# Part of the down projection as seven block products instead of eight, with wide weight tiles

## The chip, the cores and the metric

The kernel runs on one core of one Trainium2 chip. The metric is device microseconds of one execution of the whole program. The matrix engine is TensorE (PE, with its weight loads as PEld), VectorE is DVE, ScalarE is ACT, GpSimd is POOL, SyncE is SP. SP issues almost all transfers of this kernel.

## The reference, cut to what matters

Two layers of an encoder on 256 tokens of width 2048, all in float32. The change sits in the last line of a layer:

```
x = x + mixed @ w_o
x = x + (silu(g) * u) @ w_down          # [g | u] = DWConv3(RMSNorm(x) @ w_up)
```

`w_up` is 2048 x 11264 and `w_down` is 5632 x 2048 for each layer. So the down projection contracts 44 tiles of 128 features, for two tiles of 128 tokens (m = 0, 1) and four column blocks of 512 (c = 0 to 3).

## The kernel before, in words

**Products.** TensorE takes float32r operands. To keep float32 accuracy each operand is split in a rounded part (hi) and the rest (lo), and a product is three matmuls: activation hi by weight hi, activation lo by weight hi, activation hi by weight lo. `rows_by_cols` (L163) does this for one block of four 128-feature tiles by 512 columns: 4 x 2 x 3 = 24 matmuls of 128x512 into two PSUM banks, one for each token tile.

**Weights.** `split_weights` (L113) loads such a block, 1 MB, into a `raw` tile (SP, L119), makes its hi with ScalarE (L127) and its lo with VectorE, raw minus hi (`lo_part`, L111). hi and lo tiles hold 1024 columns, so a block has two of each. There are 3 raw tiles, 4 hi and 4 lo: two blocks of hi and lo, one being used and one being made. All this is urgent: the framework's scheduler puts it in its engine's queue as early as the tiles come free, and every engine then works through its queue in order. A transfer into a raw tile waits until the lo that reads the tile's old content is done; a hi or lo waits until TensorE has used the tile's old content.

**The feed-forward part.** Its 5632 features go in two halves of 24 and 20 tiles (loop at L845). For a half, `gate_and_up` (L814) takes four feature tiles at a time: four `w_up` blocks for g and four for u; the rows leave PSUM through ScalarE (`leave`, L794), are transposed by four DMA transposes on SP (L809), joined (L381), convolved (L781 to L785), gated (L827) and split in hi and lo (L242, L243) into the list `ys`, one tile of 2 KB for each feature tile. Then the down projection of that half runs at L855 to L866: for each c, one pair of PSUM banks, all blocks of the half in order, then `residual` (L560) adds the result to `xr`. The last transposes and convolutions of a half lie beside the first blocks of its down projection. `let_in` (L156) admits the steps that wait for them at the second tile of every block.

Other tiles (`sl`) come from a pool of 58 tiles of 2 KB; PSUM has three double banks (`mm`) and two single ones (`tp`).

Of the kernel before, what the change touches and what calls it, by code (L numbers as in the profile page):

```python
# [8 lines left out]
F32 = mybir.dt.float32  # L9
# [25 lines left out]

C_N1, C_AG, C_SG, C_N2, C_CW = 0, 16, 24, 32, 48
# [6 lines left out]
def encoder(ctx: ExitStack, tc: tile.TileContext, xT, x, w_in, w_gu, w_o, w_up, w_down, wsT, pcol, prow, rope, out):  # L43
# [4 lines left out]
    slots = pool("slots", 58)  # L48
    evp = pool("evp", 4)
    rawp = pool("rawp", 3)  # L50
    hip = pool("hip", 4)
    lop = pool("lop", 4)
# [56 lines left out]

    def lo_part(lo, part, hi):  # L110
        nc.vector.tensor_tensor(out=lo, in0=part, in1=hi.bitcast(F32), op=ALU.subtract)  # L111

    def split_weights(src, loaded=None, later=None, step=2 * W):  # L113
        n = src.shape[-1]
        with urgent():
            raw = loaded
            if raw is None:
                raw = rawp.tile([P, 4 * W], F32, tag="raw", name="raw")
                nc.sync.dma_start(raw[:, :n], src)  # L119
            his, los = [], []  # L120
            for h in range(0, n, 2 * W):
                hi = hip.tile([P, 2 * W], F32R, tag="hi", name="hi")
                lo = lop.tile([P, 2 * W], F32R, tag="lo", name="lo") if later is None else None
                for a in range(0, 2 * W, step):
                    part = raw[:, h + a : h + a + step]
                    cs = slice(a, a + step)
                    nc.scalar.activation(hi[:, cs], part, AF.Copy)  # L127
                    if later is None:
                        lo_part(lo[:, cs], part, hi[:, cs])
                    else:  # L130
                        later.append((part, hi[:, cs]))
                his.append(hi)
                los.append(lo)
        return his, los


    def split_later(later):
        los = []
        with urgent():
            for part, hi in later:  # L140
                lo = lop.tile([P, 2 * W], F32R, tag="lo", name="lo")
                lo_part(lo, part, hi)
                los.append(lo)
        return los
# [18 lines left out]
    def rows_by_cols(ps, acts, src, first, last, raw=None, apart=False):  # L163

        his, los = split_weights(src, raw, None, 2 * W if raw is None else W)

        def product(m, kk, part):
            cs = slice(kk % 2 * W, (kk % 2 + 1) * W)
            w = (his if part < 2 else los)[kk // 2][:, cs]
# [19 lines left out]

    def take(steps):  # L190
        for step in steps:
            with tc.issue_after(latest()):
                step()


    def unit(acts, w, steps=()):
        ps = mm()
        his, los = [], []
        for b in range(0, NK, UB):
            h, lo = split_weights(w[:, b * UW : (b + UB) * UW])  # L200
            his += h
            los += lo

        def tile_of(tiles, k, i):
            c = k % KB * UW + i * P
            return tiles[k // KB][:, c : c + P]
# [362 lines left out]
    for l in range(DEPTH):  # L569
# [244 lines left out]
        def gate_and_up(j, ys):  # L814
# [5 lines left out]
            def up_in(tall):  # L820
                for i in range(2):
# [6 lines left out]
                    for k in range(2):  # L828
                        ys.append(split_plain(y[:, k, :]))

# [14 lines left out]
        for f0, f1 in ((0, 24), (24, NF)):  # L845
            ys = []
            for j in range(f0 // 4, f1 // 4):
                gate_and_up(j, ys)
# [6 lines left out]
            for c in range(4):  # L855
                end = last and not more and c == 3
                ps = [tp([P, W]) for _ in range(2)] if end else (lambda t: [t[:, m, :] for m in range(2)])(mm())
                for k in range(f0, f1, KB):
                    src = w_down[l, c, :, k * W : (k + KB) * W]
                    rows_by_cols(ps, ys[k - f0 : k - f0 + KB], src, k == f0, k + KB == f1, None, end and k + KB == f1)  # L860
                if not (last and not more):
# [4 lines left out]
                    continue  # L866
                for m in range(2):
                    step = W // 2 if end and m else W
                    for a in range(0, W, step):
# [3 lines left out]
                        (nc.scalar if end and a else nc.sync).dma_start(out[:, m, c * W + a : c * W + a + step], to)  # L873

# [56 lines left out]
```

## Time and profile before

| | |
|---|---|
| time, median of 3 runs | 1972.02 us (1971.8 to 1972.1) |
| the profiled execution | 1971.57 us, of which its span is 1969.8 us |
| PE, busy | 1963.6 us |
| ACT, busy | 1316.6 us |
| DVE, busy | 1256.4 us |
| POOL, busy | 22.6 us |
| HBM read | 378.43 MB |

The span is what the profile covers, from the first instruction to the last; 1.8 us of the execution lie outside it. Busy time is the union of an engine's instructions. A row of the groups gives line, engine, operation, output and input, shapes and count, then busy time and mean of one, then the idle time just ahead of these instructions and what ended it.

### The profile page before, as it was taken

The page shows a single profiled execution, that of the slowest core. Times are in us where ns is not written, and L with a number is a line of the kernel's source. Part 1 is how long each engine was busy: PE and PEld are TensorE (multiplying, and loading weights), DVE is VectorE, ACT ScalarE, POOL GpSimd, SP SyncE. Part 2 cuts the span into 40 slices and gives each one's busy share as a digit, 9 for nine tenths or more (in the row PEclk, how much of TensorE's full clock was granted, in tenths as well). Part 3 has the DMA queues.
Part 4 walks back from the last instruction along what each step waited for, and adds up shares of the span by engine and source line. Part 5 has one row for each costly group of instructions (what it writes and reads, how often), then busy time and mean ns, then how long its engine had stood idle before and what let it go on. Part 6 is the DMA issues. An engine that isn't in the chain of part 4 may idle for free.

```text
span 1969.8 us, 23916 instructions
## 1 busy us (share of the span) xinstructions
PE 1963.6 (100%) x8880; PEld 1630.6 (83%) x8880; DVE 1256.4 (64%) x1754; ACT 1316.6 (67%) x1685; POOL 22.6 (1%) x25
## 2 busy tenths in 40 slices
PE   9999999999999999999999999999999999999999
PEld 8888888888888888888888888888888888888887
DVE  6779776666664456666567796666666544666664
ACT  6687487877753477777666864787777435777742
POOL 0100000000000000000000000000000000000000
PEclk9999999999999999999999999999999999999999
DMA  9764687777755677776667456867776556678763
GB/s 342 205 204 150 205 239 202 222 219 228 216 198 192 199 215 204 229 221 205 215 204 248 141 178 203 235 206 218 232 218 219 193 192 203 213 216 217 220 216 126
DMA packets 190741, 414.09 MB, mean 210 GB/s; under 512 B 139424, under 2 KB 140704, under 8 KB 145568
## 3 DMA queue, kind: packets, MB, share of 16 engines
q1 hardware_dynamic: 189904, 411.83, 67.2%
q8 instruction: 69, 1.13, 0.2%
q10 hardware_dynamic: 720, 0.73, 0.1%
q14 instruction: 48, 0.39, 0.1%
HBM read 378.43 MB, written 2.10 MB: 193 GB/s over the span
## 4 chain that ended last, share of the span: by engine, by line
PE 97%; DVE 2%; issue 0%; DMA 0%; SPq 0%; POOL 0%; ACT 0%; DVEq 0%
PE mm L170 91%; PE mm L211 2%; PE tp L170 1%; PE mm L216 1%; DVE lo L111 1%; PE tp L254 0%; PE tp L256 0%; PE tp L255 0%; PE tp L697 0%; PE tp L482 0%; DMA raw<-in_w_in 0%; DVE sl L235 0%; DVE xr L562 0%; SPq L87 0%; DVE sl L265 0%
## 5 line engine op out<-in xcount | busy, mean ns | idle before, releaser
L170 PE MATMUL mm<-hi,sl 128*128 128x512 f32 x5296 | 1418.4, 389 | 0.8 <-DVE sl L243 0.6
L111 DVE TENSOR_TENSOR lo<-raw,hi 128x1024 fp32r<-128x1024 f32 (+1 forms) x708 | 856.5, 1217 | 627.6 <-ACT hi L127 616.7
L170 PEld LDWEIGHTS mm<-hi,sl 128*128 128x128 f32 x5296 | 992.7, 188 | 208.2 <-DVE sl L243 1.5
L127 ACT ACTIVATE hi<-raw 128x1024 fp32r<-128x1024 f32 (+1 forms) x708 | 739.9, 1051 | 461.5 <-PE mm L170 426.0
L170 PE MATMUL mm<-lo,sl 128*128 128x512 f32 x2648 | 816.1, 389 | 0.0
L170 PEld LDWEIGHTS mm<-lo,sl 128*128 128x128 f32 x2648 | 496.9, 188 | 103.1
L381 ACT COPY sl<-sl 128x1024 uint16<-128x1024 uint16 x98 | 132.1, 1351 | 119.3 <-DMA sl<-sl 119.2
L781 ACT ACTIVATE sc<-sl,pc 128x256 f32<-128x256 f32 x176 | 97.0, 588 | 0.0
L801 ACT COPY sl<-ev 128x1024 uint16<-128x1024 uint16 x88 | 89.5, 1037 | 0.0
L782 DVE SCALAR_TENSOR_TENSOR sc<-sl,pc,sc 128x255 f32<-128x255 f32 x176 | 79.1, 479 | 2.6 <-ACT sc L781 2.6
L785 DVE SCALAR_TENSOR_TENSOR sc<-sl,pc,sc 128x255 f32<-128x255 f32 x176 | 79.1, 480 | 1.6
L211 PE MATMUL mm<-sl,hi 128*128 128x512 f32 x256 | 62.0, 391 | 0.0
L211 PEld LDWEIGHTS mm<-sl,hi 128*128 128x128 f32 x256 | 47.3, 188 | 9.3
L799 ACT ACTIVATE ev<-mm,yr 128x512 f32<-128x512 f32 x88 | 54.8, 672 | 0.0
L235 DVE SCALAR_TENSOR_TENSOR sl<-sl,pc 128x256 fp32r<-128x256 f32 x96 | 42.5, 479 | 16.9 <-ACT sl L234 16.9
L242 ACT ACTIVATE sl<-sl 128x256 fp32r<-128x256 f32 x88 | 32.1, 410 | 27.9 <-DVE sl L827 27.4
L234 ACT ACTIVATE sl<-sl,pc 128x256 fp32r<-128x256 f32 x96 | 43.0, 496 | 1.2 <-DMA pc<-in_pcol 0.6
L535 ACT COPY sl<-sl 128x1024 uint16<-128x1024 uint16 x24 | 32.4, 1349 | 6.8 <-DMA sl<-sl 6.8
L216 PE MATMUL mm<-sl,lo 128*128 128x256 f32 x256 | 34.2, 285 | 0.0
L243 DVE TENSOR_TENSOR sl<-sl 128x256 fp32r<-128x256 f32 x88 | 33.3, 419 | 0.0
L216 PEld LDWEIGHTS mm<-sl,lo 128*128 128x128 f32 x256 | 32.4, 191 | 0.6
L827 DVE TENSOR_TENSOR sl<-sl,sc 128x512 f32<-128x512 f32 x44 | 30.2, 686 | 0.2
(112 smaller groups left out, 582.7 us busy)
## 6 DMA issues: line engine op xcount, KB each, us to landing
raw<-in_w_up SPq DMA_DIRECT2D x176, 1024.0 KB, 5.0
raw<-in_w_down SPq DMA_DIRECT2D x88, 1024.0 KB, 4.9
raw<-in_w_in SPq DMA_DIRECT2D x38, 1024.0 KB, 5.3
raw<-in_w_o SPq DMA_DIRECT2D x32, 1024.0 KB, 5.0
raw<-in_w_gu SPq DMA_DIRECT2D x16, 1024.0 KB, 5.1
sl<-sl SPq DMA_TRANSPOSE x244, 3.6
sl<-in_prow SPq DMA_DIRECT2D x12, 256.0 KB, 7.0
raw<-in_w_in SPq DMA_DIRECT2D x8, 256.0 KB, 4.9
```

The costliest lines, as they stand in the source:

```text
L111: nc.vector.tensor_tensor(out=lo, in0=part, in1=hi.bitcast(F32), op=ALU.subtract)
L127: nc.scalar.activation(hi[:, cs], part, AF.Copy)
L170: nc.tensor.matmul(ps[m], acts[kk][:, part % 2, m * P : (m + 1) * P], w, start=first and kk == 0 and part == 0, stop=last and kk == KB - 1 ...
L211: nc.tensor.matmul(ps[:, i, :], tile_of(his, k, i), x1, start=k == 0, stop=False)
L216: nc.tensor.matmul(ps[:, i, :SEQ], tile_of(los, k, i), acts[k][:, 0, :], start=False, stop=k == NK - 1)
L234: nc.scalar.activation(t[:, 0, :], src, AF.Copy, scale=g)
L381: nc.scalar.copy(words, tall.rearrange("p (b a) n -> p b (a n)", b=2))
L781: nc.scalar.activation(t[:, i, :], s[:, i, :], AF.Identity, bias=col(3), scale=col(1))
L782: nc.vector.scalar_tensor_tensor(out=t[:, i, 1:], in0=s[:, i, : SEQ - 1], scalar=col(0), in1=t[:, i, 1:], op0=ALU.mult, op1=ALU.add)
L785: nc.vector.scalar_tensor_tensor(out=t[:, i, : SEQ - 1], in0=s[:, i, 1:], scalar=col(2), in1=t[:, i, : SEQ - 1], op0=ALU.mult, op1=ALU.add)
L799: nc.scalar.activation(rows, ps[:, m, :], AF.Copy, scale=r2[:, m : m + 1])
L801: nc.scalar.copy(h, rows.bitcast(U16).rearrange("p (j n b) -> p j b n", j=2, b=2))
```

## The change

**Seven products for eight.** Two feature tiles (k, k+1) by two token tiles by two column blocks (c, c+1) are eight block products, that is 24 matmuls. After the change some of these groups are done as seven products of sums and differences (the Winograd form of Strassen's scheme), 21 matmuls, in the new function `seven`. The halves are now 20 and 24 feature tiles. Column blocks are taken in pairs; in both pairs of the first half three groups, in the first pair of the second half four groups are done in this way, in the second pair of the second half none: ten a layer, twenty in all. All other blocks (`direct`) are as before, with 4 feature tiles, or 2 where the count leaves a rest.

**Sums of weights.** A group needs its weights and four sums of them. Of the four weight blocks (here named by their place in the row of `w_down`: 0, 1, 2, 3) three are loaded into a raw tile, the fourth twice into a second raw tile `sums`; a transfer issued by GpSimd then adds blocks 1 and 2 from HBM to these two copies as it writes (`accum_op`), and VectorE makes the other two sums. So a group has a hi and a lo of 1536 columns and another hi and lo of 2048. The host orders `w_down` so that each block's or group's weights are contiguous in a row.

**Sums of activations.** `mixed` makes four combinations of the two token tiles by two feature tiles, with three VectorE instructions, and splits them into hi and lo: seven times a layer.

**Results.** Four of the seven products go to four more PSUM banks (one `mm` and the two `tp`), which add up over all groups of a pair; `seven_out` combines them at the end of the pair's last group, with one ScalarE copy and seven VectorE instructions, into `xr`.

**Tiles.** hi and lo are 2048 columns wide everywhere, three of each (24 KB each for a partition, 16 KB before); raw tiles are four; `sl` tiles are 48. Outside the first two blocks of the program hi and lo are made with one instruction each for 2048 columns.

```diff
+HALVES = ((0, 20), (20, NF))
+FAST = ((4, 8, 14), (4, 8, 14, 18))
...
+    plain = [k for k in range(f0, f1) if k - f0 - (k - f0) % 2 not in fast]
+    out = []
+    for i in range(0, len(plain), KB):
+        ks = tuple(plain[i : i + KB])
+        own = [((c[0],), ks, False), ((c[1],), ks, False)]
+        if i // KB < len(fast):
+            k = f0 + fast[i // KB]
+            own.insert(1 if i + KB < len(plain) else 0, (c, (k, k + 1), True))
+        out += own
...
-    slots = pool("slots", 58)
+    slots = pool("slots", 48)
...
-    rawp = pool("rawp", 3)
-    hip = pool("hip", 4)
-    lop = pool("lop", 4)
+    rawp = pool("rawp", 4)
+    hip = pool("hip", 3)
+    lop = pool("lop", 3)
...
-    def split_weights(src, loaded=None, later=None, step=2 * W):
+    def split_weights(src, loaded=None, step=4 * W):
...
+            hi, lo = hi_tile(), lo_tile()
+            for a in range(0, n, step):
+                cs = slice(a, min(a + step, n))
+                nc.scalar.activation(hi[:, cs], raw[:, cs], AF.Copy)
+                lo_part(lo[:, cs], raw[:, cs], hi[:, cs])
...
+    def mixed(y):
+        t = y.rearrange("p a (m t) -> p (a m) t", t=P)
+        e = ev().rearrange("p a (m t) -> p (a m) t", t=P)
+        a21 = t[:, 1:2, :].to_broadcast([P, 2, P])
+        nc.vector.tensor_tensor(out=e[:, 0:2, :], in0=a21, in1=t[:, 0:4:3, :], op=ALU.subtract)
+        nc.vector.tensor_tensor(out=e[:, 2, :], in0=t[:, 0, :], in1=e[:, 1, :], op=ALU.subtract)
+        nc.vector.tensor_tensor(out=e[:, 3, :], in0=t[:, 2, :], in1=e[:, 2, :], op=ALU.subtract)
+        return parts(e.rearrange("p a t -> p (a t)"), [P, W])
+
+    def seven(left, right, more, acts, mix, src, used_left, used_right, first, last):
+        with urgent():
+            raw, sums = raw_tile(), raw_tile()
+            nc.sync.dma_start(raw[:, : 3 * W], src[:, : 3 * W])
+            s = sums.rearrange("p (g c) -> p g c", c=W)
+            b12 = src[:, 3 * W :].unsqueeze(1).to_broadcast([P, 2, W])
+            nc.sync.dma_start(s[:, :2, :], b12)
+            nc.gpsimd.dma_start(sums[:, : 2 * W], src[:, W : 3 * W], accum_op=ALU.add)
+            hi, lo, his, los = hi_tile(), lo_tile(), hi_tile(), lo_tile()
+            nc.scalar.activation(hi[:, : 3 * W], raw[:, : 3 * W], AF.Copy)
+            b = raw.rearrange("p (g c) -> p g c", c=W)
+            nc.vector.tensor_tensor(out=s[:, 2, :], in0=s[:, 0, :], in1=b[:, 2, :], op=ALU.add)
+            nc.vector.tensor_tensor(out=s[:, 3, :], in0=s[:, 2, :], in1=b[:, 0, :], op=ALU.add)
+            nc.scalar.activation(his, sums, AF.Copy)
+            lo_part(lo[:, : 3 * W], raw[:, : 3 * W], hi[:, : 3 * W])
+            lo_part(los, sums, his)
...
+        for ps, used, m, a, w, g in (
+            (left, used_left, 0, own(1, 0), (hi, lo), 0),
+            (right, used_right, 0, mix_of(3), (hi, lo), 2),
+            (more, used_more, 0, own(0, 0), (hi, lo), 1),
+            (more, used_more, 1, mix_of(2), (his, los), 2),
+            (more, used_more, 2, mix_of(1), (his, los), 0),
+            (more, used_more, 3, mix_of(0), (his, los), 1),
+            (left, used_left, 1, own(1, 1), (his, los), 3),
+        ):
+            cs = slice(g * W, (g + 1) * W)
+            new = m not in used
+            used.add(m)
+            nc.tensor.matmul(ps[m], a[0], w[0][:, cs], start=new, stop=False)
+            nc.tensor.matmul(ps[m], a[1], w[0][:, cs], start=False, stop=False)
+            nc.tensor.matmul(ps[m], a[0], w[1][:, cs], start=False, stop=ps is more and last)
...
-        for f0, f1 in ((0, 24), (24, NF)):
-            ys = []
+        for half, (f0, f1) in enumerate(HALVES):
+            ys, mixes = [], {}
...
+            for group in range(2):
+                fast = sevens(half, group)
+                blocks = down_blocks(half, group)
+                sums, fresh = {}, {}
...
+        "w_down": down(a(w_down)),
```

**Where the order moves: SP, start of the first half's down projection, layer 0.** SP's queue from the last `w_up` load on. Before, `raw_4684`, `raw_4722`, `raw_4756` and `raw_4790` are the first four down blocks; the transposes are those of the last up blocks.

```order
L119 DMA raw_4684<-in_w_down 128x2048
L809 DMA_TRANSPOSE sl_4526<-sl_4520 128x4x128
L809 DMA_TRANSPOSE sl_4526<-sl_4524 128x4x128
L809 DMA_TRANSPOSE sl_4527<-sl_4520 128x4x128
L809 DMA_TRANSPOSE sl_4527<-sl_4524 128x4x128
L119 DMA raw_4722<-in_w_down 128x2048
L119 DMA raw_4756<-in_w_down 128x2048
L119 DMA raw_4790<-in_w_down 128x2048
```

Now, `raw_4094` and `raw_4124` are the second and third direct block, `raw_4154` the weights of the second group of seven; `raw_4059` and `raw_4155` are the sums of the first and second group.

```order
L249 DMA raw_4059<-in_w_down 128x2x512
L918 DMA_TRANSPOSE sl_3878<-sl_3872 128x4x128
L918 DMA_TRANSPOSE sl_3879<-sl_3872 128x4x128
L918 DMA_TRANSPOSE sl_3878<-sl_3876 128x4x128
L918 DMA_TRANSPOSE sl_3879<-sl_3876 128x4x128
L156 DMA raw_4094<-in_w_down 128x2048
L156 DMA raw_4124<-in_w_down 128x2048
L246 DMA raw_4154<-in_w_down 128x1536
L918 DMA_TRANSPOSE sl_4017<-sl_4011 128x4x128
L918 DMA_TRANSPOSE sl_4018<-sl_4011 128x4x128
L249 DMA raw_4155<-in_w_down 128x2x512
L918 DMA_TRANSPOSE sl_4017<-sl_4015 128x4x128
```

Both sums stand in the same raw tile: `raw_4155` takes the place of `raw_4059`, and its transfer waits for the lo that is made of `raw_4059`. Two transposes of the last up block now stand ahead of it on SP.

**VectorE, the same place.** Before, the los of the first down blocks stand in a row, each waiting for its hi alone.

```order
L111 TENSOR_TENSOR lo_4687<-raw_4684,hi_4686 128x1024
L111 TENSOR_TENSOR lo_4691<-raw_4684,hi_4690 128x1024
L111 TENSOR_TENSOR lo_4725<-raw_4722,hi_4724 128x1024
L111 TENSOR_TENSOR lo_4729<-raw_4722,hi_4728 128x1024
L111 TENSOR_TENSOR lo_4759<-raw_4756,hi_4758 128x1024
```

Now, from the second group's sums on, in the order of the queue:

```order
L254 TENSOR_TENSOR raw_4155<-raw_4155,raw_4154 128x512
L148 TENSOR_TENSOR lo_4160<-raw_4154,hi_4159 128x1536
L255 TENSOR_TENSOR raw_4155<-raw_4155,raw_4154 128x512
L891 SCALAR_TENSOR_TENSOR sc_4219<-sl_4208,pc_89,sc_4219 128x255 x2
L894 SCALAR_TENSOR_TENSOR sc_4219<-sl_4208,pc_89,sc_4219 128x255 x2
L891 SCALAR_TENSOR_TENSOR sc_4236<-sl_3995,pc_89,sc_4236 128x255
L936 TENSOR_TENSOR sl_4210<-sl_4210,sc_4219 128x512
L894 SCALAR_TENSOR_TENSOR sc_4236<-sl_3995,pc_89,sc_4236 128x255
L148 TENSOR_TENSOR lo_4162<-raw_4155,hi_4161 128x2048
```

L254 is the first instruction that needs the accumulating transfer; the los behind it wait with it, and six convolution rows and a gating row (L936) stand ahead of the lo of the sums.

**VectorE, third and fourth group of the second half, first pair (layer 1; layer 0 has the same order).** `raw_14361` and `raw_14427` are the sums of the third and fourth group; `lo_14399` is the lo of the one direct block that TensorE does between them.

```order
L254 TENSOR_TENSOR raw_14361<-raw_14361,raw_14360 128x512
L148 TENSOR_TENSOR lo_14366<-raw_14360,hi_14365 128x1536
L255 TENSOR_TENSOR raw_14361<-raw_14361,raw_14360 128x512
L148 TENSOR_TENSOR lo_14368<-raw_14361,hi_14367 128x2048
L254 TENSOR_TENSOR raw_14427<-raw_14427,raw_14426 128x512
L148 TENSOR_TENSOR lo_14399<-raw_14396,hi_14398 128x2048
L255 TENSOR_TENSOR raw_14427<-raw_14427,raw_14426 128x512
L148 TENSOR_TENSOR lo_14432<-raw_14426,hi_14431 128x1536
```

The fourth group's first sum stands ahead of the lo of the direct block that comes before that group on TensorE. `raw_14427` takes the place of `raw_14360`, so its transfer waits for the third group's L255 and `lo_14366`.

156 lines of the change are left out of this document (115 added, 41 removed).

## The prediction

> **What bounds the kernel now.** I read the head of the page first, with the chain that ended last.
>
> ```profile
> PE 1963.6 (100%) x8880; PEld 1630.6 (83%) x8880; DVE 1256.4 (64%) x1754; ACT 1316.6 (67%) x1685; POOL 22.6 (1%) x25
> ...
> PE 97%; DVE 2%; issue 0%; DMA 0%; SPq 0%; POOL 0%; ACT 0%; DVEq 0%
> ```
>
> TensorE is busy all the time and is the chain. A busy TensorE need not be at its pace, so the next view is the chain in order of time in an undisturbed stretch, then the busy time in a stretch of the first down projection.
>
> ```profile
> 299.88 160.25 PE mm L170 x707
> ```
>
> ```profile
> 520.00:640.00 120.00, 120.00 (x531) 99.37 (x531) 68.32 (x74) 59.99 (x67) 0.00 (x0) 1.00 0.61 205
> ```
>
> A matmul of 128x512 takes 160.25 / 707 = 0.2267 us, and the down projection has the same pace: 120.00 / 531 = 0.226. The columns after it are PEld, DVE (57%), ACT (50%), POOL, the granted clock (1.00), the share of the DMA engines (0.61) and GB/s. No other engine is near its limit there. The waits tell how the feeding works.
>
> ```profile
> DVE lo L111 <- ACT hi L127: 616.7, 399, 6.2
> ACT hi L127 <- PE mm L170: 426.0, 302, 2.6
> ...
> SPq L119 <- DVE lo L111: 1212.1, 258, 14.6
> ```
>
> SP waits for a raw tile, ScalarE for TensorE to give a hi back, VectorE for ScalarE. These waits are slack: everything is made a block ahead. So fewer matmuls shorten the program, and anything that uses up the slack lengthens it.
>
> **The matmuls taken away.** Each group of seven has 21 matmuls for 24; twenty groups take away 60, 60 x 0.2267 = 13.6 us. Nothing else runs on TensorE for it. This is all that can be won.
>
> **Work added on the other engines.** The means by shape:
>
> ```profile
> L111 DVE TENSOR_TENSOR lo<-raw,hi 128x1024 fp32r<-128x1024 f32 x700 | 851.1, 1223 | 625.5 <-ACT hi L127 614.7 <-PE mm L170 9.8 <-PE mm L216 0.4
> L127 ACT ACTIVATE hi<-raw 128x1024 fp32r<-128x1024 f32 x700 | 734.8, 1056 | 459.6 <-PE mm L170 426.0 <-PE tp L170 10.0 <-PE mm L211 6.7
> ...
> L560 DVE TENSOR_TENSOR xr<-mm,xr 128x512 f32<-128x512 f32 x24 | 15.5, 686 | 10.7 <-PE mm L170 10.7
> ...
> L111 DVE TENSOR_TENSOR lo<-raw,hi 128x512 fp32r<-128x512 f32 x8 | 5.4, 692 | 2.0 <-ACT hi L127 2.0
> ...
> L127 ACT ACTIVATE hi<-raw 128x512 fp32r<-128x512 f32 x8 | 5.1, 633 | 1.9 <-DMA raw<-in_w_in 1.8
> ```
>
> 512 more columns cost a lo 1.223 - 0.692 = 0.53 us and a hi 0.42 us. So a lo of 1536 columns takes 1.75, of 2048 2.29; a hi of 1536 takes 1.48, of 2048 1.90; a sum of 128x512 takes 0.69. In the steady pattern (a group, two direct blocks) TensorE needs (21 + 48) x 0.2267 = 15.64 us. VectorE does 2 x 2.29 for the blocks and 2 x 0.69 + 1.75 + 2.29 for the group, 10.0 us or 64%; ScalarE 2 x 1.90 + 1.48 + 1.90 = 7.2 us, 46%. The transfers write 2 x 1024 KB and 768 + 512 + 512 KB, 251 GB/s beside the 205 at share 0.61 above, so about 0.75. Nobody is full. The four instructions of `mixed` on VectorE (14 x at most 4 x 0.69) and the seven of `seven_out` (six times, 5.4 us) lie beside matmuls; I cost them at nothing. If that cover failed at the six ends of a pair, TensorE would wait at most for the PSUM banks, but a direct block of 5.4 us always stands between.
>
> **The chain of a group's sums** is what has no cover by rule: a transfer into `sums` (call it B), the accumulating transfer (A), L254, the lo of 1536 columns where it stands between, L255, the hi (1.90), the lo (2.29); and only then may the next group's B start, in the same tile. That is A + B + 0.69 + 1.75 + 0.69 + 1.90 + 2.29 = A + B + 7.32 against TensorE's 15.64. Neither A nor B is in the trace. The nearest rows:
>
> ```profile
> raw<-in_w_down SPq DMA_DIRECT2D x88, 1024.0 KB, 4.9
> ...
> sl<-sl SPq DMA_TRANSPOSE x244, 3.6
> ...
> xr<-in_x SPq DMA_DIRECT2D x2, 1024.0 KB, 9.3
> out_x<-xr SPq DMA_DIRECT2D x7, 256.0 KB, 2.8
> ```
>
> Between 256 KB in 2.8 and 1024 KB in 4.9 us, B's 512 KB are at 3.5. A moves 512 KB too, but reads its destination beside its source: between 3.5 (as if plain) and 4.9 (the reading of 1 MB), I take 4.2. A + B = 7.7. From below they can't be under two transfers of 256 KB, 5.6; from above A could be as slow as the `xr` loads among other traffic, 9.3, and the sum 12.8.
>
> The Trainium skill, "DMA: Bandwidth & Descriptors", section "Anatomy of one DMA — SWDGE (gpsimd) path", gives a transfer issued by GpSimd 2.0 us and its bytes at 436 GB/s; for 512 KB that is an estimate of 3.2, A + B would be 6.7, and the forecast below about 1960. No run here shows it, and the page doesn't say that its fit covers accumulation.
>
> **Where the chain meets TensorE.** Let D be the end of the half's last up block. The two places rest on these rows:
>
> ```profile
> 532.02 5.95 SPq L809 DMA_TRANSPOSE sl<-sl  x4
> ```
>
> ```profile
> L801 ACT COPY sl<-ev 128x1024 uint16<-128x1024 uint16 x88 | 89.5, 1037 | 0.0
> L782 DVE SCALAR_TENSOR_TENSOR sc<-sl,pc,sc 128x255 f32<-128x255 f32 x176 | 79.1, 479 | 2.6 <-ACT sc L781 2.6
> ...
> L799 ACT ACTIVATE ev<-mm,yr 128x512 f32<-128x512 f32 x88 | 54.8, 672 | 0.0
> ...
> L827 DVE TENSOR_TENSOR sl<-sl,sc 128x512 f32<-128x512 f32 x44 | 30.2, 686 | 0.2
> ```
>
> First group: its B takes an up block's tile, free four blocks of 5.44 ahead of D and 1.90 + 2.29 later, D - 17.6; the sums are there before D. Its hi waits for TensorE until D, its lo is done at D + 4.2 and wanted at D + 5.44 + 2.5: no wait. Second group: B stands on SP behind two transposes (1.49 each) whose source ScalarE makes after the first group's hi (D + 1.90), two rows of 0.67 and one of 1.04: it starts at D + 7.3. Landed with A + B at 15.0; L254, lo, L255 to 18.1; six convolution rows and a gating row, 3.6, to 21.7; lo to 23.95. TensorE reaches the group at 5.44 + 4.76 + 10.88 = 21.1 and needs this lo eleven matmuls later, at 23.6. It waits 0.4 us, in four halves: 1.5. Third group: its lo is ready 15.0 after the second's, TensorE comes 15.64 after: no wait. In the first halves the later groups have more room (four short blocks lie between the third and fourth).
>
> Third to fourth group of the second half: one direct block lies between, and the order puts L254 of the fourth group ahead of that block's lo. Queued behind this L254 are that lo and all that VectorE does next, and TensorE waits for the lo at once. B may start when the third group's L255 is done, 10.8 after the second group's lo; A + B = 7.7, L254 0.69, lo 2.29: 21.5. TensorE wants it at 2.27 + 10.88 + 4.76 + 0.91 = 18.8. It waits 2.7, in two layers: 5.4.
>
> **Wide tiles at the start.** The first block after the two preloaded ones is fed straight from its transfer:
>
> ```profile
> 15.10 1.06 ACT L127 ACTIVATE hi<-raw 128x1024 fp32r<-128x1024 f32 x1 [1.69 <-DMA raw<-in_w_in]
> ...
> 16.84 1.07 PE L170 MATMUL mm<-hi,sl 128*128 128x512 f32 x4
> ...
> 17.75 0.62 PE L170 MATMUL mm<-lo,sl 128*128 128x512 f32 x2
> ```
>
> Hi would be done at 15.10 + 1.90 = 17.0, lo at 19.3, used at 17.75 before: 1.5 us late. Later blocks have three tiles instead of two blocks' worth, so more lead; I cost them at nothing.
>
> **Sum.** -13.6 + 1.5 + 1.5 + 5.4 = -5.2 us. The profiled execution took 1971.57 us (span 1969.8), 0.45 below the median of the runs; I take the difference from the median, 1972.0: 1966.8 us, 0.26% less. A difference of 0.2%, 3.9 us, is about what a measurement of this kernel can tell from none.
>
> **Rivals.**
>
> *The accumulating transfer is slow and becomes the bound; slower.* With x = A + B, the wait at the second group is x - 7.3 (four times), at the third x - 8.3 (four times), at the block between third and fourth x - 4.4 (twice). At x = 8.3 all is given back; at x = 10, 10.8 + 6.8 + 11.2 + 1.5 - 13.6 = +16.7, 1988.7; at the upper bound 12.8 it would be about 2017. For it: the four raw loads round A share the engines with it, and nothing in the trace accumulates. Against it: the share of 0.61 leaves room. Chance 0.26.
>
> *Given back, no change.* x between 7.9 and 8.7, inside my own uncertainty: 1968 to 1976. Chance 0.17.
>
> *GpSimd is held up by VectorE.* The trace has a sign of it:
>
> ```profile
> 56.08 2.99 POOL L271 TENSOR_TENSOR kr<-kv,mhalf 128x4 f32<-128x4 f32 x1 [2.74 <-DVE kv L269]
> ...
> 151.50 0.70 POOL L679 TENSOR_TENSOR lnr<-lnv,mhalf 128x2 f32<-128x2 f32 x1 [54.55 <-DVE rec L470]
> ```
>
> ```profile
> 56.12 0.42 DVE L388 TENSOR_TENSOR sl<-sl 128x256 f32<-128x256 f32 x1
> 56.45 1.22 DVE L111 TENSOR_TENSOR lo<-raw,hi 128x1024 fp32r<-128x1024 f32 x1
> ```
>
> A tiny instruction on GpSimd took 2.99 instead of 0.70 us while VectorE worked with two inputs from SBUF. If preparing a transfer is held up so, A grows by 2.3, x is 10.0: 1988.7. The Trainium skill, "SBUF — State Buffer", section "SBUF: two separate sides", has this as a trap for transfers issued by GpSimd, but for VectorE's two-port modes; its section "Who interferes with whom" says that an instruction with two SBUF inputs holds up GpSimd's reads, not its writes. By that rule the trace agrees with the row above and A stays as it is. Chance 0.06.
>
> *The attention loses.* Order and tiles change there (48 for 58), and VectorE is fuller:
>
> ```profile
> 1010.00:1170.00 160.00, 159.62 (x819) 135.44 (x818) 122.42 (x224) 114.12 (x174) 8.54 (x5) 1.00 0.59 191
> ```
>
> If four wide los a layer stood where one of half the width stood ahead of a step that TensorE waits for, 4 x 1.06 x 2 = 8.5 us: 1975.3. Against: TensorE idles 0.4 us of 160 there now. Chance 0.04.
>
> **How the numbers follow.** My forecast has 0.47; "faster" is this case, "same" is the second rival, 0.17; "slower" the other three, 0.36. The range goes from no wait at all, 1972.0 - 13.6 = 1958.4, to x = 10, 1988.7; above it lie the worst of the accumulation, about one in ten.
>
> **What would show it.** PE with 8820 matmuls at 0.227. A row of GpSimd's transfers with the time to landing, near 4.2, and of the 512 KB loads, near 3.5. VectorE's L254 waiting for a transfer; TensorE waiting for lo in each half's second group, under half a us, and some 3 us between the third and fourth group of the second halves. Near 14 us the start, with 1.5 us lost. I am wrong if TensorE waits elsewhere, or if L254 never waits.

## The result, and the profile after

The changed kernel takes 2081.5 us (median; 2076.8 to 2085.0) against 1971.9 of the kernel before on the same chip: a ratio of 1.0555, interval 1.0536 to 1.0573, 5.6% slower. The prediction was 1966.8, its range ended at 1988.7. The profiled execution of after took 2084.99 us, its span is 2083.2.

The head of the page of after and its chain that ended last:

```profile
PE 1997.3 (96%) x8820; PEld 1633.4 (78%) x8820; DVE 1326.1 (64%) x1566; ACT 1305.6 (63%) x1379; POOL 37.1 (2%) x45
...
PE 5%; DMA 1%; DVE 1%; issue 0%; ACT 0%; SPq 0%; DVEq 0%; ACTq 0%; POOLq 0%
```

The 60 matmuls are gone (8820), but TensorE is busy 33.7 us longer than before and idle for 85.9 us (2083.2 - 1997.3) where it was 6.2. So there are two losses: some 80 us of waiting, and 33.7 + 13.6 = 47 us of slower matmuls. VectorE and ScalarE are far from full, 64% and 63%.

Where it is lost, by busy time in four stretches of after: a down projection, the up projection behind it, and two more down projections, each cut at TensorE's first matmul of a stage. The columns are length, PE, PEld, DVE, ACT, POOL, granted clock, DMA share, GB/s.

```profile
497.70:627.80 130.10, 115.40 (x463) 91.04 (x463) 85.11 (x82) 63.08 (x54) 4.35 (x5) 0.93 0.69 212
627.80:899.70 271.90, 264.86 (x1154) 215.25 (x1153) 162.34 (x178) 180.17 (x187) 0.85 (x1) 1.00 0.69 202
899.70:1048.70 149.00, 135.58 (x566) 109.64 (x565) 90.59 (x83) 88.99 (x88) 2.62 (x3) 0.93 0.71 221
...
1534.20:1665.30 131.10, 114.75 (x463) 91.34 (x462) 87.25 (x84) 64.11 (x54) 4.30 (x5) 0.93 0.69 211
```

463 matmuls at 0.2267 us are 105.0 us: the first half's down projection needs 25 more, with 14.7 us of idle time and a mean clock of 0.93. But the up projection, which holds no group, takes 271.9 for 1154 x 0.2267 = 261.6 too, at full clock; in the other layer (1665.2 to 1930.0) it takes 264.8.

The waits of after, for VectorE, ScalarE and TensorE (us in all, times, longest):

```profile
DVE raw L254 <- DMA raw<-in_w_down: 118.5, 20, 10.6
```

```profile
ACT sl L490 <- DMA sl<-sl: 218.6, 47, 8.4
...
ACT hi L256 <- DVE raw L255: 128.8, 16, 10.9
```

```profile
PE mm L281 <- DVE lo L148: 34.7, 14, 4.4
PE mm L214 <- DVE lo L148: 21.6, 11, 6.9
PE mm L187 <- DVE lo L148: 18.2, 20, 2.0
```

VectorE's first sum waits for the transfer in all twenty groups, ScalarE's hi of the sums stands behind it, and TensorE waits for lo: in groups (L281), in direct blocks (L214), and in the stages outside the down projection, the up projections above all (L187), where no sum is made.

The transfers of after, with the median from issue to landing:

```profile
raw<-in_w_down SPq DMA_DIRECT2D x64, 1024.0 KB, 5.3
...
raw<-in_w_down SPq DMA_DIRECT2D x20, 768.0 KB, 4.2
raw<-in_w_down SPq DMA_DIRECT2D x28, 512.0 KB, 3.8
raw<-in_w_down POOLq DMA_DIRECT2D x20, 512.0 KB, 7.8
```

A loop of the sums, the second group of the first half, in the timelines of SP, GpSimd, VectorE and TensorE. Its load B was issued at 508.08, its transfer A at 512.62.

```profile
508.08 0.52 SPq L249 DMA_DIRECT2D raw<-in_w_down  x1
...
531.20 0.38 SPq L249 DMA_DIRECT2D raw<-in_w_down  x1
...
554.35 0.38 SPq L249 DMA_DIRECT2D raw<-in_w_down  x1
```

```profile
512.62 0.87 POOL L250 DMA_DIRECT2D raw<-in_w_down  x1 [22.55 <-DMA raw<-in_w_down]
```

```profile
523.05 0.69 DVE L254 TENSOR_TENSOR raw<-raw 128x512 f32<-128x512 f32 x1 [10.30 <-DMA raw<-in_w_down]
523.65 1.75 DVE L148 TENSOR_TENSOR lo<-raw,hi 128x1536 fp32r<-128x1536 f32 x1
525.32 0.68 DVE L255 TENSOR_TENSOR raw<-raw 128x512 f32<-128x512 f32 x1
...
528.90 2.28 DVE L148 TENSOR_TENSOR lo<-raw,hi 128x2048 fp32r<-128x2048 f32 x1
```

```profile
520.95 0.39 PE L280 MATMUL mm<-hi,sl 128*128 128x512 f32 x1
525.46 0.67 PE L281 MATMUL mm<-lo,sl 128*128 128x512 f32 x1 [4.13 <-DVE lo L148]
525.92 0.63 PE L279 MATMUL mm<-hi,sl 128*128 128x512 f32 x1
...
531.23 0.50 PE L281 MATMUL mm<-lo,sl 128*128 128x512 f32 x1 [1.86 <-DVE lo L148]
531.57 0.40 PE L279 MATMUL tp<-hi,sl 128*128 128x512 f32 x1
```

From B to A 4.5 us, from A to L254 10.4, from L254 to the end of the last lo 8.1: then the next B goes out (531.20), 23.1 us after the one before, where TensorE needs 15.64 for a group and two blocks. This is the prediction's loop, at A + B = 15.0. TensorE waits 4.13 us for the lo of 1536 columns, though its hi was done at 515.4: it stands behind the late sum on VectorE.

### The profile page after: what moved, and what is told of

It is laid out like the page before. It is cut to its first block, busy times and chain, and to the rows that moved or that the text cites. A ratio compares the mean times of both kernels' runs of the same rounds, so it can differ in the third digit from the quotient of the medians.

```text
span 2083.2 us, 22991 instructions
## 1 busy us (share of the span) xinstructions
PE 1997.3 (96%) x8820; PEld 1633.4 (78%) x8820; DVE 1326.1 (64%) x1566; ACT 1305.6 (63%) x1379; POOL 37.1 (2%) x45
## 3 DMA queue, kind: packets, MB, share of 16 engines
q8 instruction: 69, 1.13, 0.2%
## 5 line engine op out<-in xcount | busy, mean ns | idle before, releaser
L148 DVE TENSOR_TENSOR lo<-raw,hi 128x2048 fp32r<-128x2048 f32 (+3 forms) x382 | 839.7, 2204 | 421.8 <-ACT hi L160 396.0
L187 PE MATMUL mm<-hi,sl 128*128 128x512 f32 x3968 | 1067.0, 390 | 3.3 <-ACT hi L160 3.1
L187 PEld LDWEIGHTS mm<-hi,sl 128*128 128x128 f32 x3968 | 743.1, 188 | 161.6 <-ACT hi L160 7.2
L160 ACT ACTIVATE hi<-raw 128x2048 fp32r<-128x2048 f32 (+2 forms) x342 | 635.1, 1861 | 323.3 <-PE mm L187 190.1
L187 PE MATMUL mm<-lo,sl 128*128 128x512 f32 x1984 | 615.0, 391 | 18.3 <-DVE lo L148 18.2
L187 PEld LDWEIGHTS mm<-lo,sl 128*128 128x128 f32 x1984 | 370.3, 188 | 104.2 <-DVE lo L148 28.9
L214 PE MATMUL mm<-hi,sl 128*128 128x512 f32 x992 | 271.4, 396 | 0.0
L490 ACT COPY sl<-sl 128x1024 uint16<-128x1024 uint16 x98 | 129.5, 1347 | 218.6 <-DMA sl<-sl 218.6
L214 PEld LDWEIGHTS mm<-hi,sl 128*128 128x128 f32 x992 | 190.2, 192 | 41.7 <-ACT hi L160 1.0
L214 PE MATMUL mm<-lo,sl 128*128 128x512 f32 x496 | 156.4, 397 | 21.6 <-DVE lo L148 21.6
L214 PEld LDWEIGHTS mm<-lo,sl 128*128 128x128 f32 x496 | 93.9, 192 | 45.9 <-DVE lo L148 26.9
L256 ACT ACTIVATE hi<-raw 128x2048 fp32r<-128x2048 f32 x20 | 38.2, 1911 | 128.8 <-DVE raw L255 128.8
L254 DVE TENSOR_TENSOR raw<-raw 128x512 f32<-128x512 f32 x20 | 13.8, 692 | 118.5 <-DMA raw<-in_w_down 118.5
L281 PE MATMUL mm<-lo,sl 128*128 128x512 f32 x100 | 46.6, 466 | 34.7 <-DVE lo L148 34.7
L281 PEld LDWEIGHTS mm<-lo,sl 128*128 128x128 f32 x100 | 21.5, 215 | 46.3 <-DVE lo L148 42.0
```

What stands on the lines that cost most here:

```text
L160: nc.scalar.activation(hi[:, cs], raw[:, cs], AF.Copy)
L187: nc.tensor.matmul(ps[m], acts[kk][:, part % 2, m * P : (m + 1) * P], w, start=first and kk == 0 and part == 0, stop=last and kk == KB - 1 ...
L214: nc.tensor.matmul(ps[m], acts[kk][:, part % 2, m * P : (m + 1) * P], w, start=first, stop=done and kk == len(acts) - 1 and part == 2,)
L281: nc.tensor.matmul(ps[m], a[0], w[1][:, cs], start=False, stop=ps is more and last)
L490: nc.scalar.copy(words, tall.rearrange("p (b a) n -> p b (a n)", b=2))
```

## The experiments

Two theories stood at first. **Theory 1**: the loss is the loop of the sums. **Theory 2**: more than half of it comes from the wide tiles and what goes with them. Its figure of 2 to 3 us per four feature tiles was read from the times at which ScalarE empties PSUM in the up stages; that reading turns out too high: in the up projection of the 271.9 us TensorE idles 7.0 us in six such steps, 1.2 each. In the expectations the four weight blocks of a group in the order of the row are b21, b11, b22 and b12, so B loads b12 (the first expectation and the third call it b22, a slip).

**Without groups.** The wide tiles, the pools and the order of after stay.

```diff
-FAST = ((4, 8, 14), (4, 8, 14, 18))
+FAST = ((), ())
```

> The kernel after with no group of seven (all blocks of the down projection direct, 8880 matmuls as before), its wide tiles, halves, pools and order kept. Theory 1 (the loss is the loop of the groups' sums: load of b22, accumulating transfer, two adds, hi, lo): without groups nothing is lost, 1965 to 1980 us. Theory 2 (over half of the loss comes from what goes with the groups, the wide tiles and the pools, as the up stages lose too although they hold no group): 2015 to 2040 us, with TensorE idle 2 to 3 us per four feature tiles in the up stages.

1995.0 us, ratio 1.0118 (1.0103 to 1.0133): 23 us lost with no group at all. Both theories missed the size; theory 2 has its kind of loss, but a fifth of the whole.

> The kernel after with no group of seven, and hi and lo of a direct block made in two steps of 1024 columns inside the wide tiles. If a matmul waits because a wide hi or lo comes in one piece of 1.9 and 2.3 us (theory 2, by the size of a piece), this gives back most of what the kernel without groups loses: 1970 to 1990 us. If the loss is in the number of tiles (three wide ones instead of four narrow) or in the order of the queues, it stays within 10 us of the kernel without groups and whole pieces.

```diff
-    def split_weights(src, loaded=None, step=4 * W):
+    def split_weights(src, loaded=None, step=2 * W):
```

1991.4 us, ratio 1.0102 (1.0087 to 1.0117). The size of the pieces in which a wide tile is filled hardly counts.

**Sums on VectorE.** One load of 1 MB, no accumulating transfer:

```diff
-            nc.sync.dma_start(raw[:, : 3 * W], src[:, : 3 * W])
+            nc.sync.dma_start(raw, src)
-            nc.sync.dma_start(s[:, :2, :], b12)
-            nc.gpsimd.dma_start(sums[:, : 2 * W], src[:, W : 3 * W], accum_op=ALU.add)
+            nc.vector.tensor_tensor(out=s[:, :2, :], in0=b[:, 1:3, :], in1=b[:, 3:4, :].to_broadcast([P, 2, W]), op=ALU.add)
```

> The kernel after with all four weight sums on VectorE: one load of 1 MB for a group, one more add of 128x1024, no second load of b22 and no accumulating transfer. Theory 1: the load and the transfer took 9.7 to 16 us of the chain, one load takes some 5.5 and the add some 1.5, so the waits at the groups go nearly all: 2020 to 2045 us. Theory 2 alone (groups cost nothing, the tiles do): within 10 us of the kernel after, 2070 to 2090.

2006.7 us, ratio 1.018 (1.0163 to 1.0197): the transfers cost 74.8 us, more than theory 1 asked for. By TensorE's timeline the four down projections take 482 us where after has 560, so all of it lies there. But this kernel is still 11.7 us slower than the one without groups, which does 60 matmuls more.

**The pools alone.** The kernel before with the pools and halves of after, hi and lo as they were:

```diff
-    slots = pool("slots", 58)
+    slots = pool("slots", 48)
-    rawp = pool("rawp", 3)
+    rawp = pool("rawp", 4)
-        for f0, f1 in ((0, 24), (24, NF)):
+        for f0, f1 in ((0, 20), (20, NF)):
```

> The kernel before with the pools and halves of after (48 slots, four raw tiles, 20 and 24 feature tiles), its narrow hi and lo tiles kept. Theory 2 with the width of the tiles as the cause: within 5 us of before, 1967 to 1977. Its rival, that the smaller pool of slots or the other halves cost the time: 2000 us or more.

1972.4 us, ratio 1.0003 (0.9994 to 1.0012). Pools and halves cost nothing; the width stays as the cause.

**The adding of the transfer.** GpSimd's transfer overwrites its target.

```diff
-            nc.gpsimd.dma_start(sums[:, : 2 * W], src[:, W : 3 * W], accum_op=ALU.add)
+            nc.gpsimd.dma_start(sums[:, : 2 * W], src[:, W : 3 * W])
```

> The kernel after with GpSimd's transfer writing b11 and b22 over b12 instead of adding them (the sums come out wrong, everything else and every wait is kept). By the stages of the last runs the four down stages lose some 78 us to the transfers. If the reading, adding and writing of an accumulating transfer makes it slow, A falls from a median of 7.8 us to 4 to 5, as for a load of 512 KB, and the time to 2015 to 2045 us. If the cost is that a second transfer is started from GpSimd behind the first, A stays at 7 or more and the time at 2065 to 2085.

2050.6 us, ratio 1.0403 (1.0383 to 1.0423); its transfers land in a median of

```profile
raw<-in_w_down POOLq DMA_DIRECT2D x20, 512.0 KB, 5.4
```

for 7.8. The adding costs 2.4 us a transfer and 31 us in all. That lies between the two answers: 44 us of the transfers' cost remain when nothing is added. I put them down to a second transfer that can start only behind the first, and to what runs beside it; no run separates the two. In the four second groups of the first pairs this transfer takes 9.7 to 10.6 us from issue to landing with the adding and still 8.6 to 9.1 without, in the four third groups 5.4 to 5.6 and 3.8. So where it was slowest the adding is the smaller part.

**The lead.** Two tiles for the sums alone, paid with a raw tile and four slots:

```diff
-    slots = pool("slots", 48)
+    slots = pool("slots", 44)
-    rawp = pool("rawp", 4)
+    rawp = pool("rawp", 3)
+    sump = pool("sump", 2)
-            raw, sums = raw_tile(), raw_tile()
+            raw, sums = raw_tile(), sump.tile([P, 4 * W], F32, tag="sums", name="sums")
```

> The kernel after with two tiles kept for the sums alone (three raw tiles, 44 slots), so that the load of b12 need not wait for a raw tile that a direct block still reads. If the loss in the down stages is the lead (B + A of 9.7 to 16 us start too late), it falls from 78 us to under 25: 2010 to 2030 us. If the transfers hold the queue or VectorE whatever their lead, 2060 or more.

2004.6 us, ratio 1.0166 (1.0151 to 1.0182). The transfers are as slow as before, and yet VectorE hardly waits for them (its transfers, and its wait):

```profile
sums<-in_w_down POOLq DMA_DIRECT2D x20, 512.0 KB, 7.8
```

```profile
DVE sums L255 <- DMA raw<-in_w_down: 18.1, 7, 4.6
```

118.5 us of that wait are down to 18.1, and 77 us of the time are back, more than expected. So a slow transfer is harmless with a tile that is free early; what cost the time was that B could start only when the loop before it was done. Theory 1 holds for the down projections.

**The mixing.** The kernel with the sums on VectorE without `mixed`: the groups multiply plain activations.

```diff
-                        mixes[len(ys) - 2] = mixed(y)
+                        mixes[len(ys) - 2] = [ys[-1].rearrange("p a t -> p (a t)")] * 2
```

> The kernel with all four weight sums on VectorE, with the mixing of the activations left out (the groups multiply plain activations in place of the mixed ones, so the output is not the reference's). The mixing is 14 times three VectorE operations, a hi and a lo, in the up stages; there this kernel takes some 22 us more than the one without groups. If the mixing costs them: 1980 to 1990 us. If it lies under TensorE, as the prediction had it: within 5 us of 2006.7.

1973.9 us, ratio 1.0012 (1.0002 to 1.0021): 32.8 us less, where 22 were expected. Fourteen mixings cost 2.3 us each, though VectorE has time to spare. That is why the up projections lose time in after and not in the kernel without groups (layer 0's second: 261.1 us there, 267.7 with mixing, by TensorE's timeline). The edit takes away the work and also the tiles that a mixing holds, one `ev` and two `sl`; no run separates them. With the mixing SP waits 172.2 us for ScalarE's copies ahead of the transposes, without it 90.6.

**Narrow tiles.** Six hi and six lo tiles of 1024 columns in the memory of three wide ones, sums on VectorE:

```diff
-    hip = pool("hip", 3)
-    lop = pool("lop", 3)
+    hip = pool("hip", 6)
+    lop = pool("lop", 6)
...
-        return hip.tile([P, 4 * W], F32R, tag="hi", name="hi")
+        return hip.tile([P, 2 * W], F32R, tag="hi", name="hi")
```

> All four sums on VectorE, and six narrow hi and six narrow lo tiles of 1024 columns in place of three wide ones each (the same memory). If the width costs what it cost without groups (23 us), 1980 to 1990 us. If the narrow tiles also take away the waits that the mixing makes in the up stages, 1958 to 1972, the 13.6 us of matmuls less showing. If only the mixing's work counts, 2000 or more.

1956.9 us, ratio 0.9925 (0.991 to 0.9939), the second answer and a microsecond below its range: faster than both kernels, by 14.9 us against before. Its head, its TensorE's waits, and three stretches (down, up, down):

```profile
PE 1949.1 (100%) x8820; PEld 1619.8 (83%) x8820; DVE 1376.3 (70%) x1952; ACT 1360.6 (70%) x1745; POOL 21.9 (1%) x25
```

```profile
PE tp L126 <- DVE ones L122: 1.1, 1, 1.1
PE tp L373 <- DVE sl L368: 0.4, 1, 0.4
```

```profile
485.00:589.70 104.70, 104.70 (x463) 86.69 (x463) 91.41 (x109) 62.86 (x73) 0.00 (x0) 1.00 0.66 226
589.70:850.80 261.10, 261.10 (x1154) 216.20 (x1153) 169.68 (x232) 192.59 (x239) 0.00 (x0) 1.00 0.69 211
850.80:978.70 127.90, 127.90 (x566) 105.91 (x565) 92.14 (x109) 88.91 (x112) 0.00 (x0) 1.00 0.70 227
```

Same counts of matmuls as in after (463, 1154, 566), and no wait in any of the three. VectorE makes all four sums, is busy for 91.4 of 104.7 us in the first stretch, 87%, and TensorE waits for it nowhere. The mixing is hidden here.

**Transfers on narrow tiles**: the edit for the sums on VectorE taken back in the narrow kernel, and then with two tiles for the sums as well:

```diff
-            nc.sync.dma_start(raw, src)
+            nc.sync.dma_start(raw[:, : 3 * W], src[:, : 3 * W])
+            nc.sync.dma_start(s[:, :2, :], b12)
+            nc.gpsimd.dma_start(sums[:, : 2 * W], src[:, W : 3 * W], accum_op=ALU.add)
```

> The kernel after with six narrow hi and six narrow lo tiles in place of three wide ones each; the accumulating transfers and the four raw tiles are kept. If width and transfers cost what they cost apart (50 us for the width: 2006.7 against 1956.9; 75 us for the transfers: 2081.5 against 2006.7), 2025 to 2040 us. If the transfers cost what they do only because a wide lo stands behind every late sum, 1960 to 1985. If the late sums alone set the time of the down stages and the width comes for nothing beside them, 2055 or more.

> Narrow tiles, and two tiles kept for the sums (three raw tiles, 44 slots); the accumulating transfers are kept, so two of the four sums cost VectorE nothing. With the wide tiles the sums' own tiles gave back 77 of 124 us and the narrow tiles 50: together 1954 to 1960 us, like the narrow kernel with all sums on VectorE at 1956.9, if VectorE's adds were hidden there. Under 1953 if those adds still cost something; over 1965 if 44 slots or three raw tiles do not carry the up stages with narrow tiles.

1993.1 us, ratio 1.0103 (1.0086 to 1.012), and 1965.4 us, ratio 0.9963 (0.995 to 0.9976). The first fell between the answers, the second just past the bound of its last. In the first the transfers cost 36.2 us, half of what they cost on wide tiles; VectorE's waits for them are

```profile
DVE raw L263 <- DMA raw<-in_w_down: 67.8, 14, 9.0
DVE raw L263 <- issue: 38.9, 6, 8.9
```

so the sums are nearly as late as in after, and what differs is what a late sum holds up. TensorE's longest waits there are no longer in the groups' own lo:

```profile
PE mm L291 <- DVE xr L681: 11.2, 4, 3.6
PE mm L222 <- DVE lo L148: 8.9, 2, 4.6
```

The first stand at the start of the second pair of the first halves, where `residual` (L681) empties the PSUM banks of the first pair: on VectorE it stands, in layer 0, behind a first sum that waits 6.84 us for its transfer (542.47). The second are the direct blocks ahead of the fourth groups. The second run is 8.6 us behind the kernel with sums on VectorE, for the transfers, the raw tile or the slots: not separated.

The medians together:

| us | wide | narrow |
|---|---|---|
| no groups | 1995.0 | 1970.1 |
| groups, sums on VectorE | 2006.7 | 1956.9 |
| groups, transfers | 2081.5 (after) | 1993.1 |
| groups, transfers, own tiles for sums | 2004.6 | 1965.4 |

**Amount or width.** Two runs changed the number of tiles, the first of wide ones without groups, the second of narrow ones with them:

```diff
-    slots = pool("slots", 48)
+    slots = pool("slots", 40)
-    hip = pool("hip", 3)
-    lop = pool("lop", 3)
+    hip = pool("hip", 4)
+    lop = pool("lop", 4)
```

```diff
-    hip = pool("hip", 6)
-    lop = pool("lop", 6)
+    hip = pool("hip", 4)
+    lop = pool("lop", 4)
```

> The kernel without groups of seven (1995.0 us) with four wide hi and four wide lo tiles for three, and 40 slots for 48 to pay for them. If three wide tiles lose because they are too few (a tile comes back whole, and ScalarE stands at the hi that waits for it), a fourth gives back most of the 23 us: 1972 to 1980. If the width itself loses, as one wide hi or lo holds ScalarE or VectorE for 2 us, whatever their number: 1990 to 2000. If 40 slots are too few, 2000 or more.

> The narrow kernel with all sums on VectorE (1956.9 us) with four narrow hi and four narrow lo tiles for six, as the kernel before has them: two thirds of the memory of three wide ones. A group needs all four at once. If it is the width that matters and not the amount, it stays under 1965. If the group needs the other two for its lead, 1970 to 2000.

Four wide tiles: 2015.4 us, ratio 1.0231 (1.0212 to 1.025). Four narrow ones for six: 1967.4, ratio 0.9976 (0.9966 to 0.9985), two us over its bound. Two thirds of the memory cost 10.5 us, but are 39.3 us better than three wide tiles. The first run had eight slots less, so four more took the width apart. Three have pieces of 1024 columns and no groups, and tiles of `HW` and `LW` columns for hi and lo: six where they are narrow, three where wide. The fourth is the kernel before with the pools and halves of after, and 40 slots.

```diff
-HW, LW = 2 * W, 2 * W
+HW, LW = 4 * W, 2 * W
```

```diff
-HW, LW = 2 * W, 2 * W
+HW, LW = 2 * W, 4 * W
```

```diff
-    slots = pool("slots", 48)
+    slots = pool("slots", 40)
```

> No groups of seven, six narrow hi and six narrow lo tiles, everything else as in the kernel without groups whose wide tiles are made in pieces of 1024 columns (1991.4 us). If the tile is the cause: 1970 to 1974, as before. If something else that came with the change costs the time (layout, order, direct blocks): 1985 or more.

> The control with three wide hi tiles; lo narrow; pieces of 1024 in both. If a wide hi is the cause (ScalarE stands at the hi that waits for a whole tile to come back, and the transposed copies and gates stand behind it): 1985 to 1995. If wide lo is: 1970 to 1976.

> The control with three wide lo tiles; hi narrow; pieces of 1024 in both. If a wide hi is the cause: 1970 to 1976. If a wide lo is (VectorE stands at the lo that waits for a whole tile, which TensorE gives back only at a block's last lo matmul): 1985 to 1995. Some 1980 in both runs would mean that each adds its part.

> The kernel before with the pools and halves of after, narrow tiles (four and four) and 40 slots for 48. If 40 slots are too few, as one reading of the run with four wide tiles (2015.4) has it: 1985 or more. If slots cost nothing down to 40: 1970 to 1975, and four wide tiles are themselves no better than three.

| | us | ratio |
|---|---|---|
| both narrow | 1970.1 | 0.9993 (0.9984 to 1.0003) |
| hi wide | 1987.1 | 1.008 (1.0065 to 1.0095) |
| lo wide | 1972.8 | 1.0006 (0.9996 to 1.0015) |
| before, 40 slots | 2002.6 | 1.0158 (1.0141 to 1.0175) |

The control is at the time of before, so nothing else that the kernel without groups shares with after costs anything; the layout and order of the groups themselves are not in it. A wide hi costs 17.1 us, a wide lo 2.7, both together 21.3 (1991.4 - 1970.1). 40 slots for 48 cost 30.2 (2002.6 - 1972.4), so the run with four wide tiles tells nothing of them. ScalarE's waits, with both narrow, then with hi wide:

```profile
ACT hi L166 <- PE mm L198: 230.5, 180, 2.6
ACT hi L166 <- PE mm L225: 185.4, 118, 1.7
ACT sl L504 <- DMA sl<-sl: 120.2, 55, 6.5
```

```profile
ACT sl L504 <- DMA sl<-sl: 192.0, 60, 8.1
ACT hi L166 <- PE mm L225: 191.3, 62, 4.1
ACT hi L166 <- PE mm L198: 168.5, 86, 9.8
```

With narrow tiles ScalarE never waits more than 2.6 us for TensorE to give a hi back. A wide one comes back whole, after a block; ScalarE stands at it for up to 9.8 us, half as often and longer, and what is queued behind it (copies ahead of the transposes, copies behind them, gates) comes late: its wait for transposes grows from 120 to 192 us. That the lateness travels by these copies is how I read the rows; no run took them away alone. TensorE's waits in the kernel with wide hi agree in part:

```profile
PE mm L225 <- ACT sl L365: 4.3, 2, 3.1
PE mm L198 <- DVE xr L685: 3.8, 1, 3.8
```

The first are at the start of the first halves' down projections, for ScalarE's hi of the activations; 13 us ahead of the longer one ScalarE had stood 8.1 us at a copy that waits for transposes. The second is one wait in layer 1's output projection for VectorE, which these rows don't explain.

## Why the prediction was wrong, point by point

**Matmuls taken away: right.** 60, worth 13.6 us by the prediction; the narrow kernel with the sums on VectorE is 13.2 us under the one without groups (1970.1 - 1956.9).

**The step that failed most** is the sentence "Later blocks have three tiles instead of two blocks' worth, so more lead; I cost them at nothing." I counted blocks of lead and not the size of the piece that comes back. By the table the width costs 24.9 us without groups, 49.8 with groups, and 88.4 beside the transfers. At the start, where I did cost it, I saw half: 1.13 us in the first block after the preloaded ones, for 1.5, but 1.95 in the next one too (timeline of TensorE in after).

```profile
17.36 1.20 PE L187 MATMUL mm<-hi,sl 128*128 128x512 f32 x4
19.69 0.74 PE L187 MATMUL mm<-lo,sl 128*128 128x512 f32 x2 [1.13 <-DVE lo L148]
...
27.37 0.73 PE L187 MATMUL mm<-lo,sl 128*128 128x512 f32 x2 [1.95 <-DVE lo L148]
```

**The size of A and B: the second step that failed.** A was put at 4.2 and B at 3.5. In the twenty groups A took 5.4 to 10.7 us from issue to the first sum (the page's median to landing is 7.8), B 4.2 to 5.9 to the issue of A. The sum, 9.6 to 15.2, reaches beyond the bound of 12.8. By the medians the adding, so the reading of the destination, costs 2.4 (5.4 without it for 7.8), where I had put 0.7. In the second groups A takes 8.6 us and more without any adding, so most of the miss there is something else; I take it for the other transfers beside it, two loads of 1 MB issued at 511.29 among them, which I had named as the rival's reason. By the Trainium skill, "DMA: Bandwidth & Descriptors", section "Anatomy of one DMA — SWDGE (gpsimd) path", 512 KB would take an estimated 3.2; the measurements decide, 7.8 with the adding and 5.4 without, both among the kernel's other loads. The forecast of about 1960 that I hung on this estimate does not come out of my own terms either: with A + B = 6.7 they give 1958.4, 1.5 for the start and twice 1.7 ahead of the fourth groups, some 1963.

**The loop itself: right in kind, not in all its places.** A + B + 7.32, against TensorE's 15.64, gives waits in the second groups and between third and fourth of the second halves, and none in the third groups. In after the four second groups of the first pairs wait 5.0 to 6.5 us each and the third ones not at all. But in the second pairs of the first halves, where the prediction had no wait, as "the later groups have more room", TensorE waits 7.3 us in one layer and 6.6 in the other; A + B is 12.2 to 14.3 there.

Between third and fourth group of layer 0's second half A + B measured 4.39 + 7.89 = 12.28. The rival's formula x - 4.4 gives 7.9 us for that; the prediction's own sum (21.5 against 18.8 at x = 7.7) makes it x - 5.0, so 7.2. TensorE waited

```profile
960.25 1.22 PE L214 MATMUL mm<-lo,sl 128*128 128x512 f32 x2 [6.80 <-DVE lo L148]
```

6.80, in the direct block that the prediction named, where it expected 2.7. So the rival "the accumulating transfer is slow" is what happened in the down projections.

On narrow tiles its total comes near, by luck: there A's median is 6.6 and B is mostly 4.2 to 4.6, so x is about 11.0, and 4 x 3.7 + 4 x 2.7 + 2 x 6.6 = 38.8 us against the 36.2 measured. But the places differ. In that kernel the second groups of the first pairs wait 2.3 us in all for the 14.8 of the formula, the third ones 0.3 for 10.8, the blocks ahead of the fourth 8.9 for 13.2, and 11.2 us are the waits for PSUM banks at the start of a second pair. There the prediction had put the wait at nothing, because "a direct block of 5.4 us always stands between"; with a late sum in VectorE's queue that block was too short. With these A and B and the width at nothing I would have been at some 1997 us (1958.4 + 38.8), not 2081.

**The clock: a term that is missing.** The prediction takes every matmul at 0.2267 us. After long waits they are slower: 47 us in all, of which the last section shows the greater part.

**Work at nothing: right on narrow tiles alone.** Nobody was full: VectorE is busy for 85.1 of the 130.1 us of the first down projection. But with wide tiles the mixing, by its work or its tiles, costs 32.8 us, though the kernel with it has VectorE at 67% of its span: an average says nothing of whether a queue is free when it is needed.

**The other rivals.** The attention did lose, less than the rival had it: from TensorE's first matmul of a layer to the first of its up projections after takes 271.2 and 262.6 us, before 266.9 and 260.7, so 6 us more in two layers, of which 3.1 are the two waits at the start. The kernel without groups has nearly the same (271.1 and 262.4), so they belong to the wide tiles. For GpSimd held up by VectorE there is no sign at the issue: all twenty issuing instructions took 0.85 to 1.05 us. Whether something holds the transfer between issue and landing no run separates.

## What to carry to other kernels

Count lead by the piece that comes back, not by the blocks in the pool: when an engine works through its queue in order, one wait for a whole wide tile delays everything behind it, and three blocks of wide hi were worse than two of narrow. A two-step transfer into a shared tile is paid by when that tile comes free; give it a tile of its own, or do the sum on an engine with time to spare. Two such costs more than add up (here 49.8 us for the width and 36.2 for the transfers apart, 124.6 together), so test them apart and together before blaming either.

## What the runs showed of the hardware

**A long stall also slows the matmuls behind it.** The granted clock around the 4.13 us wait of the second group in after, in steps of 5 us:

```profile
520.00:525.00 5.00, 1.33 (x6) 0.75 (x5) 1.95 (x2) 0.00 (x0) 0.00 (x0) 1.00 0.34 83
525.00:530.00 5.00, 3.91 (x9) 2.68 (x9) 5.00 (x10) 3.30 (x4) 0.00 (x0) 0.66 0.48 157
530.00:535.00 5.00, 3.77 (x11) 3.03 (x12) 4.96 (x10) 4.97 (x6) 0.00 (x0) 0.75 0.37 105
535.00:540.00 5.00, 4.72 (x19) 3.52 (x19) 5.00 (x5) 2.92 (x4) 0.85 (x1) 0.91 0.63 102
540.00:545.00 5.00, 5.00 (x24) 4.14 (x23) 2.98 (x4) 1.00 (x1) 0.00 (x0) 1.00 0.88 328
```

After the wait the matmuls start every 0.43 us (525.46, 525.92, 526.35) for 0.227; it takes some 15 us until the clock is whole again, and a second wait falls into them. Waits of 1.1 us, such as the one at 510.6, left it at 1.00, and so did one of 2.17 (at 1537.2). All eight waits of 3.4 us or more in the down projections brought it down, to between 0.50 and 0.82 in the lowest step of 5 us; but so did two shorter ones close together, of 1.27 and 1.60 (at 592.4 and 594.8, then 0.59). In the three down projections shown above TensorE's busy time is 10.4, 7.3 and 9.8 us over its matmuls at 0.2267, the greater part of the 47 us that slower matmuls cost. The Trainium skill, "TensorE: Matmul & The Clock Gate", section "Part 1: The HAM clock gate (the "warmup" mystery)", has the clock fall to half after an idle window of about 3.4 us and return after a busy one; the trace agrees for single waits, with the eight of 3.4 to 6.9 us that bring it down and those of 1.1 and 2.17 that don't; the two of 1.27 and 1.60 show that the length of one wait isn't the whole rule. So a wait as long as these should be costed with the slow matmuls behind it, which the prediction left out.
